# One core of a hybrid encoder step: the sample's attention scores laid out by quarters of key blocks, and its filler work split over two halves of a PSUM bank

## The chip, the cores and the metric

The kernel runs on one NeuronCore of a Trainium2 chip. The metric is device time in microseconds (us) of one execution of the whole program; lower is better. Several executions were timed, and one was recorded by the hardware profiler. The engines are PE (TensorE matmuls; PEld is its weight load, which overlaps), DVE (VectorE), ACT (ScalarE), POOL (GpSimd) and SP, whose queue issues nearly all DMAs. Each engine takes its instructions strictly in the order in which the program holds them.

## The reference, cut to what matters

One encoder layer is applied to two groups with the same weights: a prompt of 2048 frames, and a sample of 8 streams with 16 new frames each, which attend to 1024 cached keys and to their own new ones. All is float32.

```python
def _attend(q, k, v, cum_q, cum_k, q_pos, k_pos):
    s = jnp.einsum('bqhd,bkhd->bhqk', q, k) * (HEAD_DIM ** -0.5)   # 8 heads of 64
    s = s + (cum_q[..., :, None] - cum_k[..., None, :])            # log-forget bias
    s = jnp.where(k_pos[None, :] <= q_pos[:, None], s, NEG_INF)
    p = jax.nn.softmax(s, axis=-1)
    return jnp.einsum('bhqk,bkhd->bqhd', p, v)

def _conv_module(u_hist, ...):          # depthwise conv of width 31, then, over 512 channels:
    mu = mean(y, -1); var = mean((y - mu) ** 2, -1)
    return silu((y - mu) * rsqrt(var + EPS) * ln_g + ln_b)

def _layer(x, ...):
    u, q, k, v, logf = _mixer_inputs(x, ...)              # adaLN, RMS norm, input projection
    mix = concat([conv_module(u), attention(q, k, v, logf)]) @ w_out
    x = x + g1 * mix
    h = _rmsnorm(x, norm2_g) * (1 + sc2) + sh2
    return x + g2 * ((silu(h @ w_gate) * (h @ w_up)) @ w_down)
```

## The kernel before, in words

The program runs through four stages: the input projections, the prompt's attention, the output projection (`project_out`), and the feed-forward network. Prompt and sample share the projections. In the attention stage they differ.

**The prompt's attention** goes through 16 steps (`STEPS`: 4 pairs of heads by 4 blocks of 512 queries). For each block of 128 keys and each head PE multiplies scores (`s`, L1016 and L1022), ACT takes the exponential (`e`, L1026), PE multiplies with the values (`pv`, L980), and POOL and DVE add up `sums`. Ahead of that, PE forms the same scores once more (`mx`, L933) for DVE to take their row maxima (`M`, L938); `mx` has two banks of PSUM. A step ends with `end_of_step`; the last one multiplies the sums out with `R<-sm,four` (L1055), DVE inverts them and divides, and SP stores `zc` to `cat_d` (L1058).

**The lane.** Beside it runs a background generator (`background`), which this text calls the lane. It owns one bank of PSUM (`bank("ss", "lane")`, 512 columns of float32). First it normalises the convolution's output over the channels (`conv_norm`, in chunks of 512 frames), then it sets up the sample (`sample_setup`: forget biases, written to `bias_d` and read back spread over rows into `S`), and then it works through the 8 streams, which this text calls batches (`sample_batch`). A batch does one thing after another:

1. PE: the scores of 512 cached keys (4 matmuls of 512 columns, one for each pair of heads, in four column groups of 32: `lane<-kc,Qbd`); DVE adds them to the bias (`S<-S,lane`); the next 512 keys, and the 16 new keys (`lane<-kS,Qbd`).
2. DVE: the maximum over all 1040 columns (`nm<-S`). ACT: the exponential with its row sum.
3. PE turns `S` in nine squares (`lane<-ident,S`), and ACT copies each turned piece from PSUM (`pT`, `pTn`).
4. PE: 36 matmuls with the values (`lane<-vc,pT`, `lane<-vn,pTn`); DVE multiplies by the inverse sum (`ob`); PE turns `ob`; DVE copies it to `catS`.

Keys and values of a batch are four loads of 1024 KB, two buffers each.

**What sets the order.** The generators are woven into the steps by counts of units. In `attention` the lane gets `int(nback * (units - quiet) / (total - quiet) / BACK) + 1 - done` turns in a step, from step `FIRST` on; a turn runs to the next `yield`. A scheduler then places the instructions by its own estimate of when they become ready, and by priority: `later(tc, by)` lowers that of the prompt's maxima by `MAXIMA_BY` and that of the lane by `BACK_BY`. The helpers `pe`, `flip`, `act`, `copy`, `dve` (all recorded under L1086) also hold each lane instruction behind the prompt's last instruction of that kind. What comes out is a fixed order for each engine.

`project_out` follows. Its eight accumulators `acc` (L1279) take all eight banks, the lane's as the last. It loads the concatenated rows (`cr<-cat_d`, L1331), splits them (`ch`, `cl`), and multiplies.

## Time and profile before

| | us |
|---|---|
| median of 3 runs (lowest, highest) | 2826.17 (2824.1, 2829.38) |
| the profiled execution | 2823.88 |
| its span in the trace | 2822.1 |
| lane begins on PE | 667.5 |
| the lane's first cached keys on PE | 944.4 |
| prompt's attention ends on PE (`R`) | 1150 to 1151 |
| lane ends, `acc` resumes | 1222.1 |

The profiled execution is 2.3 us below the median, and 1.8 us of it lie outside the span. The rows of the trace have the start, the duration, the engine, the line, the operation with output and inputs, and the count of merged instructions. In brackets stands how long the engine was idle before and what ended it. A float32 matmul has two records, so x8 stands for 4 matmuls; the turned squares have one.

### The profile page before, as it was taken

Reading aid. Unit: us, or ns where it says so; the run is one execution under the profiler, and the core shown is the slowest. Engines: PE = TensorE matmul, PEld = TensorE weight load, DVE = VectorE, ACT = ScalarE, POOL = GpSimd, SP = SyncE. Lnnn points to the kernel's source line nnn. Section 1 sums busy time; section 2 is a strip of 40 time slices with the busy share of each in tenths; the row PEclk is TensorE's granted clock in tenths of the full one; section 3 lists DMA queues with packets and bytes.
Section 4 is the critical chain, followed back from the end, with each engine's and each line's share of the span. In section 5 each row is a group of like instructions: output and inputs, shape, how many; then the busy total and the mean of one; then the engine's idle time right before and its main releaser. Section 6 shows DMA issues by size and latency. Waiting matters only on the chain.

```text
span 2822.1 us, 48016 instructions
## 1 busy us (share of the span) xinstructions
PE 2725.8 (97%) x16522; PEld 2385.6 (85%) x16522; DVE 2009.7 (71%) x3995; ACT 1241.8 (44%) x2408; POOL 488.0 (17%) x644
## 2 busy tenths in 40 slices
PE   7999999999999999789999999999999999999999
PEld 6999988864444554478999989999999999999999
DVE  2788898965556565325397989877786778776765
ACT  4543323343444344324254445444554446555552
POOL 3555411222434212014211110000000000000000
PEclk9999999989999999889999999999999999999999
DMA  8753657672424665555576869866786669787873
GB/s 326 257 181 121 196 204 267 194 204 86 148 87 122 189 193 169 192 176 166 198 250 202 295 215 313 276 222 206 235 295 205 216 206 316 245 286 253 271 255 118
DMA packets 406347, 603.48 MB, mean 214 GB/s; under 512 B 61556, under 2 KB 264468, under 8 KB 404056
## 3 DMA queue, kind: packets, MB, share of 16 engines
q1 hardware_dynamic: 405976, 600.31, 66.1%
q8 instruction: 130, 2.13, 0.3%
q14 instruction: 113, 0.93, 0.1%
q0 software_dynamic: 128, 0.11, 0.0%
HBM read 426.00 MB, written 174.25 MB: 213 GB/s over the span
## 4 chain that ended last, share of the span: by engine, by line
PE 82%; DMA 7%; DVE 6%; issue 2%; ACT 2%; POOL 1%; SPq 1%; DVEq 0%; ACTq 0%; POOLq 0%
PE z L1591 45%; PE z L514 5%; PE acc L1279 5%; PE pv L980 4%; PE lane L1086 3%; PE pa L322 3%; PE pvv L342 3%; PE pg L322 3%; PE mx L933 3%; PE s L1016 2%; PE s L1022 2%; PE sm L969 2%; DMA wraw<-w_in 1%; DVE ca L702 1%; DVE M L938 1%
## 5 line engine op out<-in xcount | busy, mean ns | idle before, releaser
L1591 PE MATMUL z<-rT,rW 128*128 128x360 f32 (+1 forms) x8316 | 1383.1, 328 | 6.2 <-DVE rW L1296 1.5
L1591 PEld LDWEIGHTS z<-rT,rW 128*128 128x128 f32 x8316 | 1378.4, 188 | 8.9 <-ACT rW L1295 2.4
L1295 ACT ACTIVATE rW<-rR 128x512 fp32r<-128x512 f32 x714 | 434.7, 616 | 394.0 <-PE z L1591 269.6
L1296 DVE TENSOR_TENSOR rW<-rR,rW 128x512 fp32r<-128x512 f32 x714 | 479.3, 676 | 167.0 <-ACT rW L1295 164.5
L702 DVE SCALAR_TENSOR_TENSOR cv<-cu,cpar,cv 128x384 f32<-128x384 f32 x580 | 311.8, 617 | 2.9 <-ACT cv L700 2.9
L938 DVE TENSOR_REDUCE M<-mx 128x1 f32<-128x512 f32 (+2 forms) x320 | 190.5, 607 | 168.8 <-PE mx L933 137.3
L1026 ACT ACTIVATE e<-s 128x512 f32<-128x512 f32 (+3 forms) x320 | 168.2, 533 | 258.6 <-PE s L1022 137.2
L514 PE MATMUL z<-hqx,wqh 128*128 128x384 f32 (+1 forms) x768 | 197.6, 333 | 0.8 <-DVE logf L349 0.8
L1295 ACT ACTIVATE rT<-traw 128x360 fp32r<-128x360 f32 (+1 forms) x315 | 149.2, 501 | 81.0 <-DMA traw<-gt_d 53.7
L1296 DVE TENSOR_TENSOR rT<-traw,rT 128x360 fp32r<-128x360 f32 (+1 forms) x315 | 158.0, 534 | 36.2 <-ACT rT L1295 35.6
L980 PE MATMUL pv<-e,V 128*64 128x512 f32 (+3 forms) x640 | 153.2, 555 | 0.0
L933 PE MATMUL mx<-K,Q 96*128 96x512 f32 (+2 forms) x320 | 141.2, 454 | 12.3 <-DVE M L938 10.7
L933 PEld LDWEIGHTS mx<-K,Q 96*128 96x128 f32 x320 | 62.0, 197 | 105.0 <-DVE M L938 52.8
L514 PEld LDWEIGHTS z<-hqx,wqh 128*128 128x128 f32 x768 | 136.1, 188 | 17.2 <-issue 12.4
L1279 PE MATMUL acc<-ch,woh 128*128 128x360 f32 (+1 forms) x384 | 127.6, 335 | 10.9 <-ACT ch L1295 5.4
L1016 PE MATMUL s<-Q,K 128*128 128x512 f32 (+3 forms) x320 | 129.8, 406 | 0.1
L1279 PE MATMUL acc<-ch,wol 128*128 128x360 f32 (+1 forms) x384 | 127.4, 332 | 0.0
L514 PE MATMUL z<-hqx,wql 128*128 128x384 f32 (+1 forms) x384 | 126.7, 330 | 0.0
L1519 DVE TENSOR_TENSOR rR<-rR 128x512 f32<-128x512 f32 (+1 forms) x136 | 93.9, 710 | 45.9 <-DMA rR<-w_down 40.9
L1279 PE MATMUL acc<-cl,woh 128*128 128x360 f32 (+1 forms) x384 | 122.1, 331 | 0.0
L1022 PE MATMUL s<-Q,K 128*128 128x512 f32 (+3 forms) x320 | 118.4, 370 | 0.0
L992 POOL TENSOR_TENSOR sums<-e,sums 128x512 f32<-128x512 f32 x72 | 95.3, 1324 | 108.1 <-ACT e L1026 100.6
(308 smaller groups left out, 3698.9 us busy)
## 6 DMA issues: line engine op xcount, KB each, us to landing
rR<-sup_d SPq DMA_DIRECT2D x176, 256.0 KB
rR<-w_gate SPq DMA_DIRECT2D x132, 256.0 KB
traw<-gt_d SPq DMA_DIRECT2D x154, 180.0 KB
rR<-w_down SPq DMA_DIRECT2D x104, 256.0 KB
rR<-sdn_d SPq DMA_DIRECT2D x96, 256.0 KB
rR<-w_up SPq DMA_DIRECT2D x88, 256.0 KB
sup_d<-rR SPq DMA_DIRECT2D x88, 256.0 KB
wa<-w_ada SPq DMA_DIRECT2D x16, 1024.0 KB
```

The costliest lines, as they stand in the source:

```text
L322: nc.tensor.matmul(pz[:, :n], w[:, m], x[:, :n], start=(c == 0 and k == 0), stop=(c == CB - 1 and k == 2))
L514: nc.tensor.matmul(z[:, :n], w[:, m], x[:, :n], start=(c == 0 and k == 0), stop=(c == CB - 1 and k == 2))
L702: self.pin(nc.vector.scalar_tensor_tensor(dst, src, w, acc[i], ALU.mult, ALU.add))
L933: self.mx.append(nc.tensor.matmul(mx[:, :w], Q2[0:AUX, h, j * P:(j + 1) * P], K2[kb][0:AUX, h, :w], start=True, stop=not diag))
L938: self.last_max = nc.vector.tensor_reduce(M[:, i, kb:kb + 1], mx[:, :w], AX.X, ALU.max)
L980: product = nc.tensor.matmul(z[0][HD * h:HD * h + HD, off:], V[kt // 4][:, kt % 4, HD * h:HD * h + HD], es[h][:, off:], start=(kt == 0), s ...
L1016: first = nc.tensor.matmul(s[:, off:], K1[kb][:, h, sl], Q1[:, h, off:], start=True, stop=False)
L1022: self.last_s = nc.tensor.matmul(s[:, off:], K2[kb][:, h, sl], Q2[:, h, off:], start=False, stop=not diag)
L1279: self.nc.tensor.matmul(z[:, :n], w[:, m], y, start=(first and i == 0 and k == 0), stop=(last and i == len(terms) - 1 and k == 2))
L1295: copy = self.nc.scalar.activation(hi, raw, AF.Copy)
L1296: engine.tensor_tensor(lo, raw, f32(hi), ALU.subtract)
L1591: nc.tensor.matmul(z, W[:, x, m], t[:, y, :w], start=(k == 0 and i == 0), stop=(k == n - 1 and i == 2))
```

## The change

- **Scores by quarters.** A block of 128 keys is cut in four quarters of 32. The 32 rows of a pair of heads (2 heads by 16 queries) now stand on the partitions of quarter `j`, and 256 columns of `S` hold a pair of heads. A batch's scores are 4 blocks of 8 matmuls of 128 columns. Each block fills one half of the bank (256 columns) and is added to `S` by DVE. The 16 new keys have their own 64 columns, on 32 partitions.
- **Maximum, exponential, sum.** Each quarter's maximum is taken, brought to one quarter by copies of 32 partitions, reduced, and copied back. ACT runs one exponential for each pair of heads. The sums of the four quarters are added by PE (`lane<-rsx,fold` and `lane<-ones,EnT`, 8 matmuls of one column).
- **Turning.** DVE turns all 1024 columns in squares of 32 with one instruction (`STREAM_TRANSPOSE ST<-S`), and the new keys with a second. PE's nine squares and ACT's three copies are gone.
- **Two halves.** Two generators share the bank: scores of batch b+1 in columns 0 to 255, values of batch b in 256 to 511, woven by `together`. The convolution's norm runs as two lanes in the same way, in chunks of 256 frames.
- **Order.** `in_turn` holds PE's lane instructions in the order in which they were written. `BACK` goes from 0.85 to 1.0, `BACK_BY` from 1000 to 100, `nback` from 237 to 234.
- **DMAs.** `bias_d` is written in four pieces of runs of 32, and spread into `S` two batches ahead with 10 DMAs for 8. The values are loaded after the batch before them has used its own.

```diff
-BACK = 0.85
-MAXIMA_BY, BACK_BY = 30, 1000
+BACK = 1.0
+MAXIMA_BY, BACK_BY = 30, 100
...
+def together(*gens):
+    live = list(gens)
+    while live:
+        live = [g for g in live if next(g, 1) is None]
+        if live:
+            yield
...
-            self.bias_d = d.tile([NS * H, PAST + QS], F32, name="bias_d")
+            self.bias_d = d.tile([4, NS * H, PAST // 4], F32, name="bias_d")
+            self.biasn_d = d.tile([NS * H, QS], F32, name="biasn_d")
...
-    def conv_norm(self, ch, sp, bank):
+    def conv_norm(self, ch, sp, bank, lane):
-        n = 512 if ch < 4 else P
+        n = 256 if ch < 8 else P
...
-        nback, done, units, scored = 232 + 5, 0, 0, AHEAD
+        nback, done, units, scored = 234, 0, 0, AHEAD
...
         bank = self.bank("ss", "lane")
+        halves = bank[:, 0:256], bank[:, 256:512]
         with self.pool(name="cn", bufs=1) as cn:
-            for ch in range(5):
...
+            def lane(i):
+                for ch in range(i, 9, 2):
+                    while ch >= 6 and self.conv_done < TT:
                         yield
+                    yield from self.conv_norm(ch, cn, halves[i], str(i))
+            for _ in together(lane(0), lane(1)):
+                self.conv_part(2, TT)
+                yield
...
         yield from self.sample_setup(bank)
+        yield from self.sample_scores(0, halves[0])
         for b in range(NS):
-            yield from self.sample_batch(b, bank)
+            yield from together(self.sample_values(b, halves[1]), *([self.sample_scores(b + 1, halves[0])] if b + 1 < NS else []))
...
+    def in_turn(self, ins):
+        if self.last_lane:
+            self.after(ins, self.last_lane)
+        self.last_lane = ins
+        return ins
     def pe(self, *args, **kw):
-        return self.late(self.nc.tensor.matmul, self.last_s)(*args, **kw)
+        return self.in_turn(self.late(self.nc.tensor.matmul, self.last_s)(*args, **kw))
...
     def next_bias(self, b):
...
-            for h in range(H):
-                self.nc.sync.dma_start(S[h * QS:(h + 1) * QS], self.bias_d[b * H + h:b * H + h + 1].broadcast_to([QS, PAST + QS]))
+            for j in range(4):
+                for h in range(2):
+                    rows = self.bias_d[j].rearrange("(s g h) k -> s h g k", s=NS, h=2)[b, h]
+                    self.nc.sync.dma_start(S[32 * j + QS * h:32 * j + QS * h + QS, :PAST].rearrange("p (g k) -> p g k", g=NP),
+                                           rows.unsqueeze(0).broadcast_to([QS, NP, PAST // 4]))
...
+    def next_values_of(self, b):
+        if b < NS:
+            vs = []
+            for c in range(2):
+                v = self.smc.tile([P, 4, DC], F32, tag="vc", name="vc")
+                self.nc.sync.dma_start(v, self.a["vc"][b, c * 512:c * 512 + 512].rearrange("(t p) e -> p t e", p=P))
+                vs.append(v)
...
-    def sample_batch(self, b, bank):
...
+    def sample_scores(self, b, bank):
         S, kS = self.S.pop(0)
...
+        for g in range(NP):
+            self.pe(bank[:32, QS * g:QS * g + QS], q(g), kS[:, g, :], start=True, stop=True, tile_position=(0, 0))
+        yield
+        self.dve("tensor_tensor", Sn, Sn, bank[:32, :NP * QS].rearrange("p (g k) -> p g k", g=NP), ALU.add)
+        self.dve("tensor_tensor", Sn, Sn, self.maskS[:32].unsqueeze(1).broadcast_to([32, NP, QS]), ALU.add)
+        yield
+        for i in range(4):
+            c, g0 = i // 2, i % 2 * 2
+            if g0 == 0:
                 kt = self.kc.pop(0)
+            for g in (g0, g0 + 1):
+                keys = kt[:, g].rearrange("p (t j k) -> p j t k", j=4, k=32)
+                for j in range(4):
+                    self.pe(bank[32 * j:32 * j + 32, (g - g0) * P:(g - g0) * P + P].rearrange("p (t k) -> p t k", k=32), q(g), keys[:, j],
+                            start=True, stop=True, tile_position=(0, 32 * j))
+            if g0:
                 self.next_keys(2 * b + c + 2)
+            yield
+            s = Sc[:, g0:g0 + 2, c]
+            self.dve("tensor_tensor", s, s, bank.rearrange("p (g k) -> p g k", g=2), ALU.add)
+            yield
...
+    def sample_values(self, b, bank):
...
+        self.dve("tensor_reduce", mx[:, :, 0], S[:, :PAST].rearrange("p (g k) -> p g k", g=NP), AX.X, ALU.max)
+        self.dve("tensor_reduce", mx[:32, :, 4], Sn, AX.X, ALU.max)
+        for j in range(1, 4):
+            self.dve("tensor_copy", mx[:32, :, j], mx[32 * j:32 * j + 32, :, 0])
+        self.dve("tensor_reduce", nm[:32], mx[:32], AX.X, ALU.max, negate=True)
+        for j in range(1, 4):
+            self.dve("tensor_copy", nm[32 * j:32 * j + 32], nm[:32])
+        self.dve("tensor_tensor", Sn, Sn, nm[:32].unsqueeze(2).broadcast_to([32, NP, QS]), ALU.add)
+        yield
+        for g in range(NP):
+            s = S[:, g * PAST // 4:(g + 1) * PAST // 4]
+            self.act(s, s, AF.Exp, bias=nm[:, g:g + 1], accum_out=rs[:, g:g + 1])
...
+        self.act(self.En[:, :, :QS], Sn, AF.Exp)
+        yield
+        self.dve("transpose", ST.rearrange("p g t r -> p (g t r)"), S[:, :PAST])
+        self.dve("transpose", EnT.rearrange("p g r -> p (g r)"), self.En.rearrange("p g k -> p (g k)"))
+        self.next_bias(b + 2)
+        yield
+        o, den = bank[:, :P], bank[:, P:P + 1]
...
+        for g in range(NP):
+            r = slice(32 * g, 32 * g + 32)
+            self.pe(den[r], self.fold, rs[:, g:g + 1], start=True, stop=False, tile_position=(0, 32 * g))
+            self.pe(den[r], EnT[:QS, g], self.ones[:QS, 0:1], start=False, stop=True, tile_position=(0, 32 * g))
+        self.next_values_of(b + 1)
```

On PE at the end of the prompt's attention and after it (`s`, `pv`, `sm` and `R` are the prompt's; `lane` is the lane, `acc` the output projection). Before, the scores of batch 5 stand behind `R`, and the rest of batches 5 to 7 in the middle of `acc`:

```order
L969 MATMUL sm<-e,ones 32x128 x2
L1086 MATMUL lane<-vn,pTn 32x128 x4
L1055 MATMUL R<-sm,four 128x512
L1086 MATMUL lane<-ident,ob 128x128
L1086 MATMUL lane<-kc,Qbd 32x512 x8
L1086 MATMUL lane<-kS,Qbd 32x16 x4
L1279 MATMUL acc<-ch,woh 128x368
```

```order
L1279 MATMUL acc<-cl,woh 128x368
L1086 MATMUL lane<-ident,S 128x128 x8
L1086 MATMUL lane<-ident,S 16x128
L1086 MATMUL lane<-vc,pT 32x128 x32
L1086 MATMUL lane<-vn,pTn 32x128 x4
L1086 MATMUL lane<-ident,ob 128x128
L1086 MATMUL lane<-kc,Qbd 32x512 x8
```

Now the same end of the attention:

```order
L988 MATMUL sm<-e,ones 32x384 x2
L988 MATMUL sm<-e,ones 32x256 x2
L988 MATMUL sm<-e,ones 32x128 x2
L1074 MATMUL R<-sm,four 128x512
L1350 MATMUL acc<-ch,woh 128x368
L1350 MATMUL acc<-ch,wol 128x368
```

No lane instruction is left behind `R`. The last one, `lane<-ident,ob` of batch 7, stands behind the first score of the last of the 16 steps, with 31 of the 320 blocks of scores still to come.

On PE in the middle of the sample's part now, behind the 36 matmuls with the values of batch 6 and the first six of its sums:

```order
L1105 MATMUL lane<-rsx,fold 32x1
L1105 MATMUL lane<-ones,EnT 32x1
L1105 MATMUL lane<-kc,Qbd 32x128 x8
L952 MATMUL mx<-K_6634,Q_6653 128x512
L952 MATMUL mx<-K_6641,Q_6653 128x512
L999 MATMUL pv<-e,V_7015 64x512 x2
```

The next batch's scores now follow the sums directly, in the other half of the bank.

On DVE in the middle of the sample's part, before (`M` are the prompt's row maxima, the lane's are the rows that write `S`):

```order
L1086 TENSOR_TENSOR S<-S,lane 128x512
L938 TENSOR_REDUCE M_6655<-mx 128x1
L1086 TENSOR_TENSOR sums<-e 128x512
L938 TENSOR_REDUCE M_6655<-mx 128x1
L942 TENSOR_REDUCE Z_6621<-M_6655 128x8
L1086 TENSOR_TENSOR S<-S,lane 128x512
```

and now, where a batch is turned:

```order
L957 TENSOR_REDUCE M_6656<-mx 128x1 x2
L1105 STREAM_TRANSPOSE ST<-S 128x1024
L1105 STREAM_TRANSPOSE EnT<-En 32x128
L957 TENSOR_REDUCE M_6656<-mx 128x1 x2
L1097 TENSOR_TENSOR zc<-zc,aR 128x512
L1105 TENSOR_TENSOR S<-S,lane 128x2x128
L957 TENSOR_REDUCE M_6656<-mx 128x1 x2
L1105 RECIPROCAL rd<-lane 128x1
L1105 TENSOR_SCALAR ob<-lane,rd 128x128
L1105 TENSOR_TENSOR S<-S,lane 128x2x128
```

Two or three lane instructions in a row now stand between the maxima, and the turning, which was PE's and ACT's, is DVE's.

More of the change, by code (lines that the diff above doesn't have):

```diff
@@ L867, in background @@
         bank = self.bank("ss", "lane")
+        halves = bank[:, 0:256], bank[:, 256:512]
         with self.pool(name="cn", bufs=1) as cn:
-            for ch in range(5):
-                if ch == 3:
-                    while self.conv_done < TT:
-                        self.conv_part(2, TT)
+            def lane(i):
+                for ch in range(i, 9, 2):
+                    while ch >= 6 and self.conv_done < TT:
                         yield
-                for _ in self.conv_norm(ch, cn, bank):
-                    self.conv_part(2, TT)
-                    yield
+                    yield from self.conv_norm(ch, cn, halves[i], str(i))
+            for _ in together(lane(0), lane(1)):
+                self.conv_part(2, TT)
+                yield
         self.LC.close()
@@ L1124, in sample_setup @@
         nc.sync.dma_start(self.maskS, a["maskS"])
-        qS = sm.tile([P, NP, P], F32, tag="S", name="qS", bufs=2)
+        qS = sm.tile([P, PAST + NP * QS], F32, tag="S", name="qS", bufs=2)[:, :NP * P].rearrange("p (g t) -> p g t", g=NP)
         nc.sync.dma_start(qS, self.qs_d)
+        self.En = sm.tile([32, NP, 32], F32, name="En")
+        nc.gpsimd.memset(self.En, 0.0)
+        self.fold = sm.tile([P, 32], F32, name="fold")
+        nc.vector.tensor_reduce(self.fold, self.ident.rearrange("p (j r) -> p r j", j=4), AX.X, ALU.add)
         nc.gpsimd.memset(self.Qbd, 0.0)
@@ L1185, in next_bias @@
             self.S.append((S, kS))
-    def sample_batch(self, b, bank):
-        nc, a, sm = self.nc, self.a, self.smp
-        S, kS = self.S.pop(0)
-        vs = []
-        for c in range(3):
-            c0, w = c * 512, (512, 512, QS)[c]
-            if c < 2:
-                kt = self.kc.pop(0)
-                v = self.smc.tile([P, 4, DC], F32, tag="vc", name="vc")
-                nc.sync.dma_start(v, a["vc"][b, c0:c0 + w].rearrange("(t p) e -> p t e", p=P))
-                vs.append(v)
-            else:
-                kt = kS
-            for g in range(NP):
-                self.pe(bank[32 * g:32 * g + 32, :w], self.Qbd[:, g, b].rearrange("p h q -> p (h q)"), kt[:, g, :],
-                        start=True, stop=True, tile_position=(0, 32 * g))
-            if c < 2:
+    def next_values_of(self, b):
[5 more added lines that the diff above has]
+                vs.append(v)
+            vn = self.smp.tile([QS, DC], F32, tag="vn", name="vn")
+            self.nc.sync.dma_start(vn, self.a["o_v"][T + b * QS:T + (b + 1) * QS, :])
+            self.vs = vs, vn
@@ new lines, in sample_scores, with q @@
+    def sample_scores(self, b, bank):
+        S, kS = self.S.pop(0)
+        Sc = S[:, :PAST].rearrange("p (g c k) -> p g c k", g=NP, c=2)
+        Sn = S[:32, PAST:].rearrange("p (g k) -> p g k", g=NP)
+        def q(g):
+            return self.Qbd[:, g, b].rearrange("p h q -> p (h q)")
+        for g in range(NP):
[7 more added lines that the diff above has]
+            if g0 == 0:
+                kt = self.kc.pop(0)
+            for g in (g0, g0 + 1):
+                keys = kt[:, g].rearrange("p (t j k) -> p j t k", j=4, k=32)
+                for j in range(4):
+                    self.pe(bank[32 * j:32 * j + 32, (g - g0) * P:(g - g0) * P + P].rearrange("p (t k) -> p t k", k=32), q(g), keys[:, j],
+                            start=True, stop=True, tile_position=(0, 32 * j))
+            if g0:
@@ L1205, in sample_batch @@
                 self.next_keys(2 * b + c + 2)
-            else:
-                self.next_bias(b + 1)
-                vn = sm.tile([QS, DC], F32, tag="vn", name="vn")
-                nc.sync.dma_start(vn, a["o_v"][T + b * QS:T + (b + 1) * QS, :])
             yield
-            self.dve("tensor_tensor", S[:, c0:c0 + w], S[:, c0:c0 + w], bank[:, :w], ALU.add)
-        self.dve("tensor_tensor", S[:, c0:], S[:, c0:], self.maskS, ALU.add)
-        nm = sm.tile([P, 1], F32, tag="nm", name="nm", bufs=2)
@@ L1214, in sample_batch @@
-        rs = sm.tile([P, 1], F32, tag="rsx", name="rsx", bufs=2)
-        self.dve("tensor_reduce", nm, S, AX.X, ALU.max, negate=True)
-        yield
-        self.act(S, S, AF.Exp, bias=nm, accum_out=rs)
-        yield
-        self.dve("reciprocal", rs, rs)
-        pts = []
-        for c in range(2):
-            pp = bank.rearrange("p (i k) -> p i k", i=4)
-            for i in range(4):
-                self.flip(pp[:, i, :], S[:, (4 * c + i) * P:(4 * c + i + 1) * P], self.ident)
-            yield
-            pT = sm.tile([P, 4, P], F32, tag="pT", name="pT", bufs=2)
-            self.copy(pT, pp)
-            pts.append(pT)
```

68 lines of the change are left out of this document (40 added, 28 removed).

## The prediction

> **What bounds the kernel now.** I read the page first, then busy time by stage, then PE's timeline at the end of the attention.
>
> ```profile
> span 2822.1 us, 48016 instructions
> PE 2725.8 (97%) x16522; PEld 2385.6 (85%) x16522; DVE 2009.7 (71%) x3995; ACT 1241.8 (44%) x2408; POOL 488.0 (17%) x644
> PEclk9999999989999999889999999999999999999999
> ```
>
> PE is busy for 97% of the span, so what counts is where PE does not work, or works slowly. Three slices of the clock show 8, two of them neighbours, from 1129 to 1270 us. The next rows are stretches of time (start:end, length, busy time of PE, PEld, DVE, ACT and, where it worked, POOL, then the granted clock, the DMA share and GB/s), first of everything, then of the lane's instructions alone.
>
> ```profile
> 944.00:1151.00 207.00, 204.82 (x1329) 99.56 (x1328) 113.40 (x202) 88.92 (x172) 47.02 (x35) 1.00 0.59 170
> 1177.00:1222.20 45.20, 25.64 (x292) 14.75 (x291) 10.49 (x24) 9.48 (x17) 0.00 (x0) 0.66 0.45 156
> ```
>
> ```profile
> 944.00:1151.00 207.00, 40.82 (x530) 18.22 (x530) 11.15 (x28) 7.11 (x15) 1.00 0.59 170
> 1177.00:1222.20 45.20, 25.58 (x291) 14.66 (x290) 5.48 (x15) 4.26 (x9) 0.66 0.45 156
> ```
>
> From 944 to 1151 the prompt's attention and batches 0 to 4 of the lane share PE, which is idle for 2.2 us of 207. From 1177 on the lane is alone: 25.58 of PE's 25.64 us are its own, at a clock of 0.66, and for 19.6 us PE does nothing. PE's timeline there, thinned:
>
> ```profile
> 1149.98 1.12 PE L1055 MATMUL R<-sm,four 128*128 128x512 f32 x2 [0.37 <-ACT sm L1050]
> ...
> 1162.94 0.67 PE L1279 MATMUL acc<-ch,woh 128*128 128x368 f32 x1 [2.83 <-ACT ch L1295]
> ...
> 1176.40 0.60 PE L1086 MATMUL lane<-ident,S 128*128 128x128 f32 x4
> 1179.25 1.06 PE L1086 MATMUL lane<-ident,S 128*128 128x128 f32 x4 [2.25 <-ACT pT L1086]
> ...
> 1206.34 1.67 PE L1086 MATMUL lane<-kc,Qbd 128*32 128x512 f32 x8 [0.81 <-DVE S L1086]
> ...
> 1212.17 1.11 PE L1086 MATMUL lane<-ident,S 128*128 128x128 f32 x4 [3.06 <-ACT S L1086]
> ...
> 1222.14 0.41 PE L1279 MATMUL acc<-ch,woh 128*128 128x368 f32 x1 [0.64 <-DVE catS L1086]
> ```
>
> At `R` the prompt is through, and three batches of eight are left. The output projection begins at 1162.94, stops at 1176.40 and resumes at 1222.14, held by the last batch's `catS`. The bound is thus PE's work up to 1150, and a chain PE, DVE, ACT, PE from 1176 to 1222.
>
> **The change part by part.**
>
> *The tail.* In the order of after no lane instruction stands behind `R`, so the stretch from 1176.40 to 1222.14 goes: -45.7 us. The gap from `R` to the first `acc` stays, since a load covers it:
>
> ```profile
> 1155.57 0.34 SPq L1058 DMA_DIRECT2D cat_d<-zc  x1
> 1156.32 0.58 SPq L1174 DMA_DIRECT2D kc<-kcT  x1
> 1156.95 2.53 SPq L1331 DMA_DIRECT2D cr<-cat_d  x4
> 1162.38 1.47 ACT L1295 ACTIVATE ch<-cr 128x368 fp32r<-128x368 f32 x3 [11.15 <-DMA cr<-cat_d]
> ```
>
> On SP's queue `cr` stands behind the last `zc`, as it does in the order of after; only the keys' load between them goes. I take -1 us for that. Nothing else is brought forward. The weights that are still missing at `R` were all split some 29 us after it, even with the lane's loads beside theirs:
>
> ```profile
> 1178.09 0.63 ACT L1295 ACTIVATE woh<-raw 128x512 fp32r<-128x512 f32 x1 [0.20 <-DMA raw<-w_out]
> ```
>
> The first of them is needed after four of eight blocks of `acc`, 13 us to the first matmul and 96 matmuls of 0.17 us (slower at first, as before) behind `R`, some 31 us. I expect no new stop there.
>
> *The three batches on PE.* Their work moves between the prompt's matmuls, where PE is full. A batch there costs 40.82 / 5 = 8.2 us by busy time, too much, since a matmul's tail overlaps the next one. From start to next start it is less:
>
> ```profile
> 944.38 1.07 PE L1086 MATMUL lane<-kc,Qbd 128*32 128x512 f32 x8
> 945.38 0.50 PE L933 MATMUL mx<-K,Q 96*128 96x512 f32 x1
> ...
> 979.69 0.65 PE L1086 MATMUL lane<-vc,pT 128*32 128x128 f32 x16
> 980.27 0.51 PE L933 MATMUL mx<-K,Q 96*128 96x512 f32 x1
> ...
> 1003.57 0.60 PE L1086 MATMUL lane<-ident,S 128*128 128x128 f32 x4
> 1003.92 0.48 PE L933 MATMUL mx<-K,Q 96*128 96x512 f32 x1
> ```
>
> Two blocks of scores 2 x 1.00, nine squares 0.8, 36 matmuls with values at 0.0725 each 2.6, new keys and `ob` 0.3: 5.7 us in whole blocks. Values in pieces cost more, since each change of kind adds about 0.1 us; the true price lies between 5.7 and 8.2. I take 6.8, near the middle: 3 x 6.8 = +20.4 us (17 to 25).
>
> *What a batch costs anew on PE.* The squares go: -0.8. The 32 narrow scores cost what narrow values cost, 32 x 0.0725 = 2.3, for 2.0 before: +0.3; two more blocks, +0.2. The four small scores of the new keys now follow each other in one column group: +0.2. Eight matmuls of one column are new; the nearest row is the weight load of such a narrow matmul:
>
> ```profile
> L1086 PEld LDWEIGHTS lane<-kS,Qbd x40: 106/108/110, 958.7 to 1120.7; 128*32 128x32 f32 x40
> L1086 PE MATMUL lane<-kS,Qbd x40: 182/193/204, 958.7 to 1120.7; 128*32 128x16 f32 x40
> ```
>
> 8 x 0.108 = 0.9 us if nothing overlaps, 0.2 if the four groups do. I take 0.6, as the pairs of weights alternate. A batch: +0.5, eight: +4 us (-4 to +10). [...]
>
> *The convolution's norm* streams the same columns in twice as many matmuls: 0 (-2 to +3).
>
> *DVE and ACT* are off the path as long as they deliver in time. ACT loses three copies and gains three exponentials' starts: 0. DVE's rows:
>
> ```profile
> L938 DVE TENSOR_REDUCE M<-mx 128x1 f32<-128x512 f32 x60 | 41.0, 688 | 37.8 <-PE mx L933 36.1 <-PE mx L937 1.3
> L1086 DVE TENSOR_TENSOR S<-S,lane 128x512 f32<-128x512 f32 x10 | 6.8, 680 | 7.7 <-PE lane L1086 4.2 <-DMA S<-bias_d 3.6
> L1086 DVE TENSOR_REDUCE nm<-S 128x1 f32<-128x1040 f32 x5 | 6.1, 1222 | 0.1
> 1151.15 3.36 DVE L1056 RECIPROCAL aR<-R 128x512 f32<-128x512 f32 x1 [1.11 <-PE R L1055]
> ```
>
> No row turns squares. A pass over as many columns is the maximum, 1.2 us; the dearest kind shown is the inverse, 6.7 us for 1024. I take 1.2, the reduction being the nearer in kind (one input, one pass). With six copies of 32 partitions and two more small passes at 0.17 and smaller adds, a batch costs DVE about 3.2 us more than the 4.2 before. Counted by the prompt's scores `s`, the sample's part now runs between the places of these two rows of before:
>
> ```profile
> 903.55 0.45 PE L1016 MATMUL s<-Q,K 128*128 128x512 f32 x1
> ...
> 1103.80 0.50 PE L1016 MATMUL s<-Q,K 128*128 128x512 f32 x1
> ```
>
> These 200 us, less some 35 of the lane, plus 8 x 6.8 make 220 us, 27.5 a batch, where five batches had 207. DVE had 113.4 of 207 us; with 7.4 us a batch, it is busy for about 70% of 27.5 us (0.53 of 20.7 us of the prompt's work, and 7.4). Cover is there, and behind a late DVE instruction stand the maxima `M`, for which `mx` and so PE wait.
>
> *DMA.* Per batch 4 x 1024 KB and 0.5 MB of biases, 4.7 MB in 27.5 us, is 171 GB/s; the prompt's own share was 170 GB/s less 5 x 4.7 MB in 207 us (114), 56. At 170 GB/s the share was 0.59, so a full share is 288, and 227 are 79%. The added biases' DMAs are hidden two batches ahead; the keys have 17 to 20 us to land.
>
> *Waits.* PE waited little for the lane within the attention:
>
> ```profile
> PE lane L1086 <- DVE S L1086: 0.5, 1, 0.5
> PE mx L933 <- DVE M L938: 0.4, 1, 0.4
> ```
>
> That is 0.2 us a batch, at 42 us a batch. Now seven hand-overs a batch, 56 in all, stand in a denser order. Bounds: 0 as here, or the tail's 0.8 us each (0.81 above), 45 us. I take 0.1 each, near the rows of the attention, where other work lies between: +6 us.
>
> *Sum*: -45.7 - 1 + 20.4 + 4 + 6 = -16.3 us. Against the profiled 2823.9 that is 2807.6, against the median of 2826.2, by which a new kernel would be timed, 2810.
>
> **The rivals.**
>
> *More is gained.* Hand-overs stay at nothing and the small matmuls hide under weights: -45.7 - 1 + 19 + 0 = -28, 2798. For it speaks PE's 2.2 us of idle time in 207; against it that the lane then had lowest priority and half again as much time.
>
> *Hand-overs decide (slower).* Both halves lie in one bank. PE writes scores while DVE reads, so that each block waits for the add before it, and in PE's fixed order the prompt's matmuls queue behind. At the tail's 0.8 us each the sum is -46.7 + 20.4 + 4 + 45 = +23, 2849; it turns from gain to loss at (46.7 - 24.4) / 56 = 0.40 us. Against it: in the attention another 2 to 4 us of PE work stand between two lane blocks, longer than DVE's 0.7 us add. A turning at 6.7 us (DVE at 87%) would bring it about. [...]
>
> *The halves bring nothing.* The lane runs as densely as the order says only if it waits about 0.4 us at each hand-over: the tail's gain is paid back within the attention, 2826.
>
> *Loads come late.* At 79% of the DMA's share a burst of the prompt's `K` and `Q` (0.5 MB each) delays keys or values by some 3 us a batch, with PE waiting at the head of its queue: +24, 2834. For it speaks that SP's queue also waits for buffers; against it that the tail fed itself at 156 GB/s without waiting for a load.
>
> **How the numbers follow.** Forecast 0.62 (2801 to 2820), more gained 0.12, hand-overs slower 0.11, halves bring nothing 0.08, loads late 0.07. The time is the forecast's, 2810. For 8 in 10, the forecast, the larger gain and the even case are needed (0.82), so 2793 to 2830. A change under 0.2% (5.7 us) can hardly be told from none. Faster 0.74, within 0.2% 0.08, slower 0.18.
>
> **What would show it.** Right: `acc` begins some 12 us behind `R` and runs on without a stop; `R` comes at about 1180; the clock's slices there stay at 9 save one; PE's busy time for the lane is 65 us in the sample's part, with under 10 us of waits for lane, `S` or `M`. Wrong: PE waiting for DVE `S`, `M` or `ST` by more than 20 us, a turning far above 1.2 us, waits for `kc` or `vc`, or new stops of `acc` for `cr` or `woh`.

## The result and the profile after

The changed kernel takes 2810.26 us (median of 4 runs, 2807.7 to 2812.26) against 2827.14 us of the kernel before in the same session (2824.1 to 2829.38). The ratio is 0.9941, with a 95% interval of 0.9923 to 0.9958. The profiled execution took 2811.56 us, 12.3 us less than the one of before, by span as by time. So the two recorded executions show 12.3 of the 16.9 us between the medians, and it is these 12.3 us that are taken apart here.

The page of the changed kernel, the three lines that answer to those of before:

```profile
span 2809.8 us, 49281 instructions
PE 2725.3 (97%) x17042; PEld 2407.4 (86%) x17042; DVE 2024.6 (72%) x4116; ACT 1234.3 (44%) x2472; POOL 495.9 (18%) x677
PEclk9999999989999999999999999999999999999999
```

PE is busy as long as before, with 520 records of matmuls more. Of the three slices of the clock with an 8, the two from 1129 to 1270 us are gone. PE's timeline at the end of the attention:

```profile
1186.12 1.13 PE L1074 MATMUL R<-sm,four 128*128 128x512 f32 x2 [0.72 <-ACT sm L1069]
1195.59 0.67 PE L1350 MATMUL acc<-ch,woh 128*128 128x368 f32 x1 [8.34 <-ACT ch L1366]
```

And a stretch of time behind it (busy time of PE, PEld, DVE, ACT, POOL, then clock, DMA share, GB/s):

```profile
1209.00:1260.00 51.00, 51.00 (x305) 51.00 (x305) 18.43 (x32) 16.86 (x32) 7.10 (x7) 1.00 0.62 208
```

`R` comes 36.1 us later than before, `acc` begins 9.5 us behind it (13.0 before), and then PE works without a pause. From the first `acc` to the span's end it is 1614.2 us, where it was 1659.2. So 36.1 - 3.5 - 45.0 = -12.4 us: the tail was worth 48.5 us, and 36.1 of them were given back within the attention.

Where they were given back can be split. The 9th and the 16th step of the prompt end with a copy `zc` on ACT, at 907.75 and 1148.10 us before, and at 907.51 and 1184.27 us now; up to 907 us the two kernels run level. Between these copies, first all instructions and then the lane's alone, of before and then of after:

```profile
907.75:1148.10 240.35, 237.82 (x1501) 118.26 (x1501) 133.63 (x247) 100.73 (x196) 57.55 (x47) 1.00 0.60 172
907.75:1148.10 240.35, 43.96 (x555) 21.06 (x555) 13.29 (x37) 7.11 (x15) 1.00 0.60 172
```

```profile
907.51:1184.27 276.76, 258.36 (x2226) 140.20 (x2226) 165.23 (x364) 104.57 (x243) 54.93 (x42) 0.96 0.57 174
907.51:1184.27 276.76, 54.87 (x1280) 39.82 (x1280) 22.24 (x72) 0.00 (x0) 0.96 0.57 174
```

Three parts add up to the stretch: the lane's time on PE (43.96, now 54.87), PE's idle time (240.35 - 237.82 = 2.53, now 18.40), and the rest, in which PE works for the prompt alone (193.86, now 203.49). The matmuls of the prompt are the same 946 in both. So the 36.4 us are 10.9 of the lane, 15.9 of idle time, and 9.6 us by which the prompt's own matmuls take longer, at a mean clock of 0.96.

Part of the 9.6 us is the clock. Before, it stands at 1.00 throughout; now it is 0.50 in four stretches, 20.5 us in all:

```profile
917.90:921.30 3.40, 3.40 (x11) 1.39 (x9) 1.08 (x2) 1.19 (x2) 0.00 (x0) 0.50 0.27 64
965.70:969.10 3.40, 3.40 (x21) 1.82 (x21) 3.23 (x13) 0.67 (x2) 0.00 (x0) 0.50 0.92 300
1016.90:1027.20 10.30, 6.15 (x29) 3.18 (x30) 3.96 (x12) 3.41 (x11) 1.27 (x1) 0.50 1.08 329
1034.00:1037.40 3.40, 3.40 (x9) 1.13 (x8) 0.63 (x2) 0.60 (x1) 0.00 (x0) 0.50 0.30 74
```

PE works in 16.35 us of them, 1.56 us of it for the lane. So 14.8 us of the prompt's work went at half the clock. If it takes twice as long there, that is an estimated 7.4 of the 9.6 us.

What PE waited for there, by the view of waits (us in total, times, longest):

```profile
PE lane L1105 <- DMA kc<-kcT: 9.3, 5, 5.5
PE lane L1105 <- DVE S L1105: 5.2, 2, 3.0
PE mx L952 <- DVE M L957: 1.9, 4, 0.9
```

The longest wait, in PE's timeline, then SP's queue ahead of it, and the stretches of time around it:

```profile
1014.82 0.42 PE L1105 MATMUL lane<-kS,Qbd 128*32 128x16 f32 x8
1020.78 1.08 PE L1105 MATMUL lane<-kc,Qbd 128*32 128x128 f32 x16 [5.54 <-DMA kc<-kcT]
```

```profile
1008.98 0.95 SPq L1233 DMA_DIRECT2D vc<-vc  x2
...
1010.56 0.61 SPq L1207 DMA_DIRECT2D kc<-kcT  x1
...
1012.08 1.49 SPq L911 DMA_DIRECT2D K<-k_d  x1
1013.62 1.06 SPq L913 DMA_DIRECT2D K<-k_d  x1
1014.72 1.24 SPq L925 DMA_DIRECT2D Q<-q_d  x1
```

```profile
1005.00:1010.00 5.00, 5.00 (x49) 3.01 (x46) 2.96 (x10) 1.11 (x3) 1.27 (x1) 1.00 0.30 89
1010.00:1015.00 5.00, 5.00 (x40) 2.27 (x39) 4.57 (x8) 2.36 (x4) 2.55 (x2) 1.00 0.92 310
1015.00:1020.00 5.00, 0.24 (x8) 0.14 (x5) 2.35 (x12) 2.22 (x9) 0.28 (x1) 0.69 1.07 362
1020.00:1025.00 5.00, 3.95 (x25) 2.59 (x25) 2.57 (x7) 0.60 (x1) 0.00 (x0) 0.50 1.09 298
```

Within 6 us SP asks for two loads of values, one of keys, and the prompt's `K` and `Q`. The DMA engines go from 0.30 of their time to all of it, and the keys, asked for at 1010.56, let PE go on at 1020.78, 10 us later. The clock falls to 0.50 within the stop and stays there until 1027.2. The second largest wait looks like a hand-over, but is not one. PE's row, and DVE's rows ahead of it:

```profile
963.80 0.42 PE L1105 MATMUL lane<-kS,Qbd 128*32 128x16 f32 x8 [3.03 <-DVE S L1105]
```

```profile
962.07 1.34 DVE L1097 TENSOR_TENSOR zc<-zc,aR 128x512 f32<-128x512 f32 x1 [3.91 <-DMA aR<-inv_d]
963.34 0.41 DVE L1105 TENSOR_TENSOR S<-S,lane 128x256 f32<-128x256 f32 x1
```

DVE stood for 3.9 us before the prompt's division, whose input `aR` had not landed, and the lane's add behind it came late.

### The profile page after: what moved, and what is told of

It reads as the page before. It is cut to its first block, busy times and chain, and to the rows that moved or that the text cites. A ratio compares the mean times of both kernels' runs of the same rounds, so it can differ in the third digit from the quotient of the medians.

```text
span 2809.8 us, 49281 instructions
## 1 busy us (share of the span) xinstructions
PE 2725.3 (97%) x17042; PEld 2407.4 (86%) x17042; DVE 2024.6 (72%) x4116; ACT 1234.3 (44%) x2472; POOL 495.9 (18%) x677
## 5 line engine op out<-in xcount | busy, mean ns | idle before, releaser
L952 PE MATMUL mx<-K,Q 96*128 96x512 f32 (+2 forms) x320 | 140.8, 455 | 10.9 <-DVE M L957 9.3
L524 PEld LDWEIGHTS z<-hqx,wqh 128*128 128x128 f32 x768 | 136.1, 188 | 15.9 <-issue 12.4
```

Source lines behind the costliest of these rows:

```text
L524: nc.tensor.matmul(z[:, :n], w[:, m], x[:, :n], start=(c == 0 and k == 0), stop=(c == CB - 1 and k == 2))
L952: self.mx.append(nc.tensor.matmul(mx[:, :w], Q2[0:AUX, h, j * P:(j + 1) * P], K2[kb][0:AUX, h, :w], start=True, stop=not diag))
```

## The experiments

The theories: (A) the gain is that the lane ends before `R`, by whatever means; (B) what was given back are loads that come in bursts, and the slow clock behind a stop; rivals are (C) hand-overs between PE and DVE, (D) that one lane can't run so densely, (E) that the layout pays by itself, (F) the new kinds of PE work, (G) the clock under narrow matmuls. Where a ratio is given, it is to the kernel before on the same chip, with its 95% interval. The split by lane, idle time and prompt is worked out for each kernel as above, between its own two copies `zc`; the tables give it in us. In the expectations of experiments 1 and 2, theory A is late loads that one more buffer cures, and theory B a full DMA share or queue, by which the stop only moves; here both belong to B.

### 1. A third buffer for the keys

```diff
-kt = self.smc.tile([P, NP, 512], F32, tag="kc", name="kc")
+kt = self.smc.tile([P, NP, 512], F32, tag="kc", name="kc", bufs=3)
...
-                self.next_keys(2 * b + c + 2)
+                self.next_keys(2 * b + c + 3)
```

> A third buffer for the cached keys; everything else as changed. Theory A (the moved batches pay most in loads that come late): PE's 9.3 us of waits for kc, the longest 5.5 us, fall under 2 us, and the slow clock behind the 5.5 us wait goes with them; R some 10 to 14 us earlier than 1186.1, ratio to before 0.989 to 0.991 (2796 to 2801 us). Theory B (the DMA share or SP's queue is the limit, so another buffer only moves the wait to biases, values or the prompt's K and Q): kc's wait goes but the same time appears elsewhere, ratio 0.994 as with two buffers. Theory C (hand-overs between PE and DVE set the pace): nothing changes, 0.994, with PE's waits for S and M still there.

Measured: 2820.66 us, ratio 0.998 (0.997 to 0.999), slower than the change. PE's timeline at the place of the wait for keys:

```profile
1023.84 1.22 PE L952 MATMUL mx<-K,Q 96*128 96x512 f32 x2 [10.93 <-DMA Q<-q_d]
```

No wait for `kc` is left, and a wait of 10.9 us for the prompt's `Q` stands at the same place. In the changed kernel, too, the first `mx` behind the stop, at 1022.13, still waits 0.27 us for `K`: the prompt's loads were late there as well. The idle time is 18.3 us, as in the changed kernel. That speaks for the burst and against C. None of the forecast ratios came (0.989 to 0.991 for a cure, 0.994 for the rest), because the lane and the prompt take 8.9 us more on PE (58.8 and 208.4). The clock, at 0.50 for 30.8 us where it was 20.5, is an estimated 2 of these; the rest is not explained.

### 2. Keys in halves, more buffers for the biases

```diff
-kt = self.smc.tile([P, NP, 512], F32, tag="kc", name="kc")
+kt = self.smc.tile([P, 2, 512], F32, tag="kc", name="kc", bufs=5)
...
-S = self.smp.tile([P, PAST + NP * QS], F32, tag="S", name="S", bufs=2)
+S = self.smp.tile([P, PAST + NP * QS], F32, tag="S", name="S", bufs=3)
```

> Keys in half loads with five buffers, and three buffers for S and the new keys, so that both keys and biases have more time to land. Theory A (late loads): the waits for kc (9.3 us) and for S behind late biases (5.2 us) both go, with the slow clock behind them; R 14 to 18 us earlier, ratio 0.987 to 0.990. Theory B (DMA share or SP's queue): more issues on the same queue, ratio 0.994 or worse, with waits for K, Q or vc in the place of kc. Theory C (hand-overs): 0.994, S waits stay at 5 us or more.

Measured: 2821.55 us, ratio 0.9985 (0.9972 to 0.9998). Again no wait for keys, 7.9 us for `Q`, 5.1 us for `S`, and 18.1 us of idle time. The forecast for a cure, 0.987 to 0.990, was wrong; that of the rival came, 0.994 or worse with a wait for `Q` in the place of `kc`. SP's queue has the values and two half loads of keys, asked for from 1009.48 to 1012.34, ahead of the prompt's `K` and `Q`, from 1012.98 to 1017.77, and further buffers change nothing in that.

### 3. The order alone

```diff
-MAXIMA_BY, BACK_BY = 30, 1000
+MAXIMA_BY, BACK_BY = 30, 100
```

in the kernel before, and nothing else.

> The kernel before with BACK_BY at 100 for 1000 and nothing else: one lane, old layout, but the last batch ends one turned square behind R. Theory A (it is density that pays; the layout and the halves are a means to it): the stretch of 45.7 us with the lane alone goes and three batches at 6.8 us or a bit more come into the attention; with one chain of 13 steps a batch PE waits some 1 us a batch more than the changed kernel does without its late loads, ratio 0.993 to 0.997. Theory D (one lane cannot run so densely: each batch's chain of PE, DVE, ACT takes the 17 us of the tail plus the prompt's work between its steps, so PE waits at every step in its fixed order): 13 waits x 8 batches x 0.4 us = 40 us, ratio 0.998 to 1.005.

Measured: 2796.82 us, ratio 0.9893 (0.9871 to 0.9914). That is better than the change, whose interval begins at 0.9923, and the best of the versions that do all the work. PE's timeline, and the two stretches (all, lane):

```profile
1166.51 1.12 PE L1055 MATMUL R<-sm,four 128*128 128x512 f32 x2
...
1177.84 0.68 PE L1279 MATMUL acc<-ch,woh 128*128 128x368 f32 x1 [5.37 <-ACT ch L1295]
```

```profile
905.45:1164.62 259.17, 249.62 (x1726) 125.02 (x1726) 143.39 (x259) 106.84 (x209) 55.15 (x42) 0.96 0.63 188
905.45:1164.62 259.17, 52.77 (x780) 27.05 (x780) 18.72 (x47) 10.50 (x22) 0.96 0.63 188
```

The last turned square, the values and `ob` of batch 7 stand just behind `R`, and the rest of the lane is within the attention. That takes 18.8 us more than before (259.17 - 240.35): lane +8.8, idle +7.0, prompt +3.0. The changed kernel pays 36.4. So A holds, though its own forecast was only 0.993 to 0.997; D (0.998 to 1.005) is refuted, and neither the layout nor the halves are needed for the gain. The clock is 0.50 for 20.5 us here as well (927.0 to 937.3 and 1114.8 to 1125.0), 10.6 of them with the prompt on PE.

### 4. Scores and values one after the other

```diff
-        yield from self.sample_scores(0, halves[0])
         for b in range(NS):
-            yield from together(self.sample_values(b, halves[1]), ...)
+            yield from self.sample_scores(b, halves[0])
+            yield from self.sample_values(b, halves[1])
```

> The changed kernel with scores and values of a batch one after the other, not woven: new layout, turning on DVE and the new order's numbers kept; about one and a half batches then stand behind R. Theory A (what pays is that the lane ends before R): a tail of some 25 us is back and 1.5 batches x 8 us leave the attention, ratio 0.996 to 1.000. Theory E (the gain comes from the layout itself, fewer instructions on PE's and ACT's path): ratio still about 0.994.

Measured: 2826.89 us, ratio 1.0001 (0.9989 to 1.0012). `R` comes at 1173.0 and the end of the lane behind it costs what was saved. E falls, A stands. In the new layout, with these order numbers, the halves are what brings the lane to its end in time.

### 5 and 6. The changed kernel with other orders

```diff
-BACK = 1.0
+BACK = 1.1
```

> The changed kernel with BACK at 1.1 for 1.0: the lane's turns stretch over more of the attention, and its last instruction stands 33 rows ahead of R for 96. Theory B (bursts of loads set what is lost): the lane asks for its loads 10% less densely, and its batches meet the bursts of K, Q and V at other places; of the 18 us in which PE is idle between 903 and 1147 about a third goes, ratio 0.990 to 0.992, the longest wait for kc under 4 us. Theory F (the new kinds of PE work, narrow scores and sums of one column, are what costs): PE does the same work, ratio 0.994. Theory C (hand-overs): fewer rows between them nowhere, 0.994, waits for S as before.

```diff
-BACK = 1.0
-MAXIMA_BY, BACK_BY = 30, 100
+BACK = 0.85
+MAXIMA_BY, BACK_BY = 30, 1000
```

> The changed kernel with BACK at 0.85 and BACK_BY at 1000 as before: layout, halves and turning stay, and about the last batch stands behind R, in the middle of acc. Theory A (what pays is that the lane ends before R): one batch's tail of 17 to 20 us comes back and some 7 us leave the attention, ratio 0.998 to 1.001. Theory E (layout and halves pay by themselves): 0.994 or less.

Measured: 0.9988 (0.9979 to 0.9998) with the lane spread, 0.9997 (0.9985 to 1.001) with the old numbers. The second is as A says. The first refutes my forecast of 0.990 to 0.992, though its idle time fell as forecast:

| kernel | stretch | lane | idle | prompt |
|---|---|---|---|---|
| changed | 276.8 | 54.9 | 18.4 | 203.5 |
| 5: spread | 291.7 | 66.8 | 10.7 | 214.2 |
| 6: old numbers | 284.1 | 65.7 | 5.9 | 212.5 |

In both, the scheduler puts the lane's narrow matmuls in small groups between the prompt's. PE's timeline of kernel 6, and two stretches right after it:

```profile
967.86 0.22 PE L1105 MATMUL lane<-rsx,fold 128*32 128x1 f32 x2
968.01 0.38 PE L1035 MATMUL s<-Q,K 128*128 128x256 f32 x1
968.32 0.22 PE L1105 MATMUL lane<-ones,EnT 16*32 16x1 f32 x2
968.47 0.38 PE L1041 MATMUL s<-Q,K 128*128 128x256 f32 x1
```

```profile
970.00:975.00 5.00, 5.00 (x28) 2.69 (x25) 1.84 (x5) 0.13 (x1) 0.00 (x0) 0.50 0.27 81
975.00:980.00 5.00, 5.00 (x14) 1.53 (x17) 1.06 (x4) 0.43 (x2) 0.00 (x0) 0.51 0.94 331
```

The lane takes 11 to 12 us more on PE, in kernel 6 with fewer records of its own in the stretch (1166 for 1280), the prompt 9 to 11. A part of that is the clock, which fell to 0.50 for some 10 us here with no stop of PE in the 11 us before. In all it is 0.50 for 27.2 us in kernel 5 and 23.8 in kernel 6, an estimated 4 to 5 us more of lost work than in the changed kernel. So the eight batches of kernel 5, which stand in pieces, cost 23 us more on PE (66.8 + 214.2 against 54.9 + 203.5): more than the whole gain. That the pieces cause the rest of it is argued from the rows, not shown by a run of its own.

### 7 and 8. The price of a batch, and of the tail

```diff
-        for b in range(NS):
+        for b in range(4):
```

> The changed kernel with four of the eight batches; batches 4 to 7 are left out. It prices a batch: R against 1186.1 us, over four. By the prediction's terms, 6.8 + 0.5 + 0.75 = 8.05 us each, R at 1154. Theory B (late loads cost most, and most of them lie in batches 0 to 3, at 916, 964 and 1021 us): 6 us each or less, R at 1162 or later, and the same waits of 3 and 5.5 us there. Theory F (PE's own new work): 7 us each by its busy time of 55 us for eight, R at 1158.

And the kernel before with `range(5)`; in both, the loads of the batches left out go too:

> The kernel before with five of the eight batches; batches 5 to 7 are left out, so that nothing of the lane stands behind R but one turned square. It prices the tail: R stays at 1150, acc begins some 10 us later and runs on; by the stretch of 45.7 us and the shorter gap the span is 2822.1 - 47 = 2775 us. Against the order alone (2797.0), the difference over three batches is then what a batch costs within the attention in the old layout: 7.3 us. If acc without the tail runs into weights or rows that come late (the rival), it stops and the span is above 2785.

Measured, one run each: spans of 2769.3 us (changed, four batches) and 2766.7 us (before, five). `R` comes at 1145.23 us with four batches, 40.9 us earlier than with eight, so that a batch costs 10.2 us. The split says of what: the lane 28.3 us for four batches, 7.1 each; idle time 9.5 (18.4 against 8.9); the prompt's matmuls 1.4; the last 1.8 us lie ahead of the 9th step's copy. None of the three forecasts for `R` came (1154, 1162 or later, 1158). F had the work right, 7 us each. B had the place wrong: the wait of 5.5 us is for the keys of batch 4, which is left out here, and no wait for `kc` is left at all. That fits the 9.5 us of idle time, which the forecast by PE's work did not have.

With five batches before, PE's timeline:

```profile
1145.37 1.13 PE L1056 MATMUL R<-sm,four 128*128 128x512 f32 x2 [0.37 <-ACT sm L1051]
1146.33 0.27 PE L1087 MATMUL lane<-ident,ob 128*128 128x128 f32 x1
1155.62 0.67 PE L1280 MATMUL acc<-ch,woh 128*128 128x368 f32 x1 [9.01 <-ACT ch L1296]
```

`acc` runs on without a stop, 10.25 us behind `R` instead of 12.96, and from there to the end it is 1611.1 us instead of 1659.2: the tail's price is 2.7 + 48.1 = 50.8 us, where 47 was forecast. Against experiment 3, with its span of 2797.0 us, the three batches more cost 30.3 us, 10.1 each, where 7.3 was expected. So by these spans a batch is no cheaper in the new layout (10.2) than in the old.

### 9. Values loaded once

```diff
         if b < NS:
+            if b:
+                return
             vs = []
```

> The changed kernel with the cached and new values of batch 0 loaded once and used for all eight batches; the loads of the other batches' values (2 MB each) are left out, PE's work is the same. Theory B (what the lane pays beyond its own work are bursts of loads, and the slow clock that follows a stop of PE): the 5.5 us wait for kc near 1015 goes, PE's idle time between the end of the 9th and the 16th step falls from 18.4 us to under 10, the time of the prompt's own matmuls there from 203.5 us towards the 194 us of before; R near 1170, ratio 0.987 to 0.990. Theory C or F (hand-overs, or PE's own new work): R within 3 us of 1186, ratio 0.993 to 0.995.

Measured: ratio 0.9907 (0.9887 to 0.9927), 9.6 us better than the change by the two ratios (0.0034 x 2826), whose intervals just overlap (0.9923 to 0.9927). The stretches (all, lane):

```profile
912.86:1178.45 265.59, 257.89 (x2226) 139.49 (x2226) 167.63 (x364) 104.29 (x243) 55.62 (x42) 0.98 0.45 125
912.86:1178.45 265.59, 54.66 (x1280) 39.63 (x1280) 22.04 (x72) 0.00 (x0) 0.98 0.45 125
```

The stretch is 11.2 us shorter, and idle time explains it: 7.7 us for 18.4. B's forecast, a ratio of 0.987 to 0.990 and `R` near 1170, was just missed: `R` comes at 1180.3, partly since the 9th step ends 5.4 us later than in the changed kernel. PE waits for no key, and once for `S`, 1.8 us at the first biases. So 10.7 us of the idle time are loads that wait for other loads, and B is shown for that part. The other part of B did not come: the prompt's matmuls take 203.2 us, as in the changed kernel, though the clock rose from 0.96 to 0.98.

### 10. Without the sums of one column

```diff
-        for g in range(NP):
-            self.pe(den[r], self.fold, rs[:, g:g + 1], ...)
-            self.pe(den[r], EnT[:QS, g], self.ones[:QS, 0:1], ...)
...
-        self.dve("reciprocal", rd, den)
+        self.dve("reciprocal", rd, self.ones[:, 0:1])
```

> The changed kernel without the eight matmuls of one column in each batch (the row sums); the division uses 1 in their place. By the prediction's term (0.6 us a batch) R comes 5 us earlier; by the changed kernel's rows (16 records at 0.15 us) 1.2 us a batch, 10 us earlier, ratio 0.990 to 0.991. Theory G (these narrow matmuls also let the clock fall, as it does without a stop of PE where they stand among other narrow ones): more than 12 us earlier, and the prompt's own matmuls take under 200 us for 203.5. If the stops for loads only become longer by what PE saves, R moves by under 3 us.

Measured: ratio 0.9936 (0.9921 to 0.995), the same as the change. The view of waits, for PE:

```profile
PE lane L1105 <- DMA kc<-kcT: 14.8, 5, 5.4
```

The lane takes 6.4 us less (48.5), and 3.4 us of that come back as idle time, 1.7 as time of the prompt; the waits for keys rise from 9.3 to 14.8 us. The last case of the expectation holds, with `R` at 1186.65: what PE saves, it waits. F falls for the changed order, and so does the price that G had set. G's claim on the clock does not fall: without the sums the mean clock of the stretch is 0.98, and its two stretches at 0.50 (967.2 to 974.0 and 1021.8 to 1028.6) both begin within stops for keys, of 5.35 and 5.05 us.

### 11. Three key buffers, values asked for later

```diff
-        self.next_values_of(b + 1)
-        yield
+        yield
         ob = ...
...
             self.dve("tensor_copy", self.catS[r, :, b, :], po[r, :, h, :])
+        self.next_values_of(b + 1)
```

> Three buffers for the keys, and the next batch's values asked for two or three turns later, behind the prompt's loads. Theory B (the burst at the change of the pair of heads is what stops PE: kc in the changed kernel, Q with three key buffers): with the values out of the burst neither kc nor Q is waited for by more than 4 us, and the ratio is 0.989 to 0.993. If values then come late themselves, PE waits for vc in their place and the ratio is 0.995 or more.

Measured: 2812.45 us, ratio 0.9951 (0.9934 to 0.9967); there are only times of this version, and no trace is used. The median meets the second forecast (0.995 or more), but the interval reaches down to 0.9934, and whether PE waits for `vc`, that forecast's reason, is not shown. Against experiment 1 (0.998, 0.997 to 0.999), the same kernel with earlier values, it is better, and the two intervals do not meet. So the place of the values' loads matters by some 8 us, but this place only leads back to the change's own time.

### 12. The turning five times over

```diff
-        self.dve("transpose", ST..., S[:, :PAST])
+        for _ in range(5):
+            self.dve("transpose", ST..., S[:, :PAST])
```

> The changed kernel with the turning of a batch done five times over (1.23 us each, so 6.1 us a batch and 39 us of DVE's time more). The prediction's rival said that a turning of 6.7 us brings the hand-overs to decide (2849 us). By that rival: PE's waits for S, M and ST rise by more than 20 us, time 2835 or more. If DVE has cover there (149.5 us busy of 244, then 189 of 244): waits rise by under 8 us, time 2810 to 2822, a part of it since the last batch then ends only at R.

Measured: 2813.28 us in one run. The groups of the tile `ST`, and the waits of PE:

```profile
L1105 DVE STREAM_TRANSPOSE ST<-S x40: 1190/1232/1247, 938.6 to 1183.2; 128x1024 f32<-128x1024 f32 x40
```

```profile
PE lane L1105 <- DVE S L1105: 9.1, 5, 3.5
PE mx L952 <- DVE M L957: 5.4, 7, 1.8
...
PE lane L1105 <- DMA kc<-kcT: 0.8, 1, 0.8
PE lane L1105 <- DVE ST L1105: 0.8, 2, 0.4
```

The waits for `S`, `M` and `ST` rise by 8.2 us, from 7.1 to 15.3, a hair more than the 8 I set and far from 20 (9.5 with the wait of `pz` for `M`, 1.3 us); those for keys fall by 8.5. The time is in the range for cover. The rival's condition, a turning of 6.7 us, was nearly met (5 x 1.23 = 6.2), and hand-overs did not decide.

## Why the prediction was right, and where it was not

The forecast, 2810 us, is the measured median, and the mechanism was the stated one: the tail goes, and part of it is given back within the attention. That it fits to the microsecond is luck. The two profiled executions differ by 12.3 us where the sum said 16.3, and in the sum waits that were 9.9 us too small stand against a tail and batches that came out 5.7 us better. Predicted and measured, in us against the profiled execution:

| term | predicted | measured |
|---|---|---|
| tail, with the shorter gap | -46.7 | -48.5 |
| three more batches, and what a batch costs anew | +24.4 | +20.5 (lane 10.9, prompt 9.6) |
| waits | +6 (hand-overs) | +15.9 (idle time) |
| sum | -16.3 | -12.1 (by span -12.3) |

**The tail.** The step was right: no stop of `acc` for `cr` or for weights came in its place. The gap behind `R` shrank by 3.5 us, where I took 1. Experiment 8 gives the tail, alone, 50.8 us.

**The batches.** 6.8 + 0.5 us of PE work for a batch was close to the 7.1 us of experiment 7. Its parts were not. The lane's whole time on PE in the sample's part is 55 us where I forecast 65. The prompt's 9.6 us had no term in the sum; the table puts them here because the price of a batch was to hold all that the moved work costs PE. They do not go with the number of batches (1.4 us for four, experiment 7), and the clock, for which the sum had no term either, is an estimated 7.4 of them. The eight matmuls of one column were mis-sized: I took 0.6 us a batch, and the timeline has each pair of records 0.15 us behind the last:

```profile
1003.67 0.22 PE L1105 MATMUL lane<-rsx,fold 128*32 128x1 f32 x2
1003.82 0.22 PE L1105 MATMUL lane<-ones,EnT 16*32 16x1 f32 x2
```

That is 1.2 us a batch, twice the term. Taken out in experiment 10, they shorten the lane's time on PE by 0.8 us a batch (6.4 / 8), and the kernel by nothing that can be told, as long as loads hold PE.

**The waits** are the step that failed. I priced 56 hand-overs at 0.1 us, and gave late loads 0.07 as a rival case with 3 us a batch. Hand-overs proper cost next to nothing: both large waits for `S` (3.03 and 2.18 us, of 7.1 for `S` and `M`) had a late load behind them, `aR` at 963.80, and the first biases at 916.10, where DVE itself waits 5.6 us for `S<-biasn_d`. Late loads made 10.7 of the 18.4 us of idle time (experiment 9), and waits for `kc`, which the prediction had named as a sign of being wrong, came with 9.3 us. My reason against that rival, that the tail fed itself at 156 GB/s, was a mean over 45 us; the burst fills the DMA engines for 15 us and more, at 298 to 362 GB/s, and 288 was what I took for a full share. The 17 to 20 us that I gave the keys were less too: the load was asked for at 1010.56 and its first user stood at the head of PE's queue by 1015.2.

**DVE.** The turning takes 1.23 us (I took 1.2, between 1.2 and 6.7), and DVE is busy for 165.2 of 276.8 us between the copies, 60% (70% forecast). Cover was there with a turning of 6.2 us as well (experiment 12).

**The halves** were behind the rival that ends slower. DVE does take turns with PE at the bank. The tile view of the keys shows who waits for their matmuls:

```profile
  DVE rd L1105: 19.2, 5
```

`rd` reads the sums in the values' half and needs no keys, yet it starts only when the scores in the other half are through. Of 72 reads of the bank by DVE in the stretch, none runs beside a matmul of the lane. Seven of the eight `rd` start some 0.07 us behind the last matmul of a block of scores, and the view puts the wait down to that matmul's semaphore, so it looks like a wait of the program's own; what the chip would do without it, no run shows. The price falls on DVE, which has time, and not on PE, so that the rival's 0.8 us each never came.

**What I did not see** is that the gain needed no new layout. No term of the sum was `BACK_BY` alone. Experiment 3 shows that this number alone is worth 1.07% (0.9893), more than all parts together (0.9941), while the new layout with the old numbers is worth nothing that can be told (experiment 6, 0.9997).

Two things stay open. The first is why the prompt's matmuls take 203.5 us in the changed kernel and 196.9 in experiment 3. The clock, at 0.50 for 14.8 and 10.6 us of the prompt's work, is an estimated 2 us of it. Nor does the rest go with the number of batches: it is 202.1 us with four batches in the new layout (experiment 7) and 193.6 with five in the old (experiment 8). The second is why a third key buffer lengthens both the lane's and the prompt's time on PE by more than the clock explains.

## What to carry to other kernels

When filler work is left over at the end of a stage, try the numbers that place it before its layout: here one priority (0.9893) did more than the whole change, with its new layout, second half-bank and new turning (0.9941). When filler is packed more densely into a stage that PE fills, look at the DMA share in slices of 5 us and at the order on the load queue, not at means (here a mean of 0.57, and slices of 0.92 to 1.09): each load of the filler stands ahead of or behind one of the main work's, and a buffer more can move the stop to the other side of the queue (experiment 1: from 5.5 us for `kc` to 10.9 us for `Q`). And a wait for an engine is read one step further back, to what that engine waited for (here 3.03 us of PE for `S`, behind 3.91 us of DVE for `aR`).

## What the runs showed of the hardware

The clock does not only fall behind a stop. In kernel 6 PE is busy for 5.00 of 5 us from 970 to 975 and from 975 to 980, with no stop in the 11 us before, and the granted clock is 0.50 and 0.51; ahead of it stand some 4 us in which matmuls of 1 to 128 columns on 32 columns of the array alternate with the prompt's short ones. The sums of one column are among them, and the traces point at these. Between the two copies `zc` of the nine traced kernels that have the sums, 16 stretches at 0.50 begin with no stop of PE over 0.5 us in the 6.8 us before; each of them has at least ten of the 16 records of a batch's sums in the 3.4 us before (as long as the shortest stretch at 0.50 of the changed kernel). In the changed kernel it is the one from 1034.0 to 1037.4. The four traced kernels without these sums (before, 3, 8 and 10) have no such stretch, though they keep other matmuls on 32 columns. The sums alone do not decide it, since those of seven batches of the changed kernel have no slow clock right behind them.

In the changed kernel the clock fell within the stop of 5.54 us ahead of 1020.78 (0.50 from 1016.9 to 1027.2). It also fell behind shorter stops, of 2.18 us ahead of 916.10 (0.50 from 917.9 to 921.3) and of 3.03 us ahead of 963.80 (0.50 from 965.7 to 969.1), and in kernel 6 an order of PE without gaps, 10.00 of 10 us busy from 970 to 980, was no protection.

A matmul of one column, with its weights, took 0.15 us from start to start in the changed kernel (1003.67 to 1003.82), as two records, 0.075 each. Each record has a weight load of its own there, 64 for the 64 records of `lane<-rsx,fold` (median 108 ns) and 64 for those of `lane<-ones,EnT` (102 ns).
